# A hybrid streaming-encoder layer on one core: softmax normalisation moved from the probabilities to the outputs, and banded operands split by head pairs

## The chip, the cores and the metric

The kernel runs on one core of a Trainium2 chip. The metric is device microseconds (us) of one execution, lower is better; the times given are medians of several executions. The core has five engines with queues of their own: TensorE (PE; its weight loads are listed apart as PEld), VectorE (DVE), ScalarE (ACT), GpSimd (POOL) and SyncE (SP, which issues most transfers). They work at the same time and wait for one another through semaphores. SBUF and PSUM are the on-chip memories; TensorE writes to PSUM, in banks of 128 partitions by 512 float32.

## What is computed

One layer over 512 positions of width 1024, in float32, chunk-causal with chunks of 64. Three branches read one input projection: A is banded softmax attention with a clipped relative-position bias, B a gated linear recurrence (HGRN2), C multi-head latent attention. A and C have 8 heads with values of width 64. Their results are multiplied by a branch matrix, gated, summed and projected; a squared-ReLU feed-forward layer and a norm follow. The change touches the two softmaxes and the operands around them:

```python
# A, one chunk of queries
s = jnp.einsum('bqhd,bkhd->bhqk', q_blk, k_band).astype(jnp.float32) * scale + bias
s = jnp.where(valid[None, None], s, -jnp.inf)
p = jax.nn.softmax(s, axis=-1).astype(v.dtype)
return jnp.einsum('bhqk,bkhd->bqhd', p, v_band)
...
# C, one block of queries
s = (jnp.einsum('bqhd,bkhd->bhqk', qn, k_nope)
     + jnp.einsum('bqhr,bkr->bhqk', qr, k_rope)).astype(jnp.float32) * scale
s = jnp.where(mask[None, None], s, -jnp.inf)
p = jax.nn.softmax(s, axis=-1).astype(v.dtype)
return jnp.einsum('bhqk,bkhd->bqhd', p, v)
```

## The kernel before

**Precision.** An operand of a float32 product is split into a high part, rounded to the format that TensorE takes (`hi`, a copy on ScalarE), and a low part, the rest (`lo`, a subtraction on VectorE); `split` (L209) does both. A product is three matmuls, high by high, high by low and low by high (`mm3`, L223).

**Order of the work.** TensorE's order is written out by hand; the other engines' instructions are put in order by a planner that goes by the program's order and by what it expects to be ready, and each engine then takes its own in that order. The large projections are cut into units, mostly of one matmul, that wait in a list; `fill(n)` (L303) puts the next n units at that place of TensorE's order. Weights come by SyncE into two raw buffers (`load`, L261), are converted by ScalarE and an accumulating transfer (`convert`, L267), and two converted tiles are kept ahead (`get`, L283). The stages are: projection of the latent parts; attention C (span 66 to 158 us); attention A (to 280 us); the recurrence B, filled with the gate and branch matmuls (to 545 us); output projection and feed-forward.

**Attention** (L567) has one loop for both softmaxes, over 8 heads by 4 tiles of 128 queries, and a few steps more to drain. Step i of head h and tile t does, in TensorE's order: the scores of (h, t) (`scores_step`, L517), some fill, at odd steps a waiting value step (`value_step`, L555), the transposes of the tile two steps back (`transpose_step`, L541), the preparation of later operands, and fill again. The score step takes the row's minimum of the negated scores (VectorE, L526, or L530 with the bias added), and the exponential with its sum (ScalarE, L533). Its `norm` takes the reciprocal of the sum (L537) and scales the row of up to 512 probabilities (L538), both on VectorE. The transposes (L546) of the scaled row go to PSUM and are split into `pT`, which covers one head's 512 queries. The value step multiplies `pT` by the values, high parts and low parts of a head side by side (L562); the two halves of its 128 output rows are added by a copy (L564, ScalarE) and a sum (L565, VectorE) into one half of the tile `ys` of the head's pair. Value steps and transposes share two PSUM banks.

**Operands of attention C** are made from the latent projections by `prep_c` in stages (L673). Three of them, at L681, L686 and L691, write to the one PSUM bank called `up` (`pup`, L165): they fall on the steps of odd heads with t = 0, 1 and 2, heads 1, 3 and 5.

**Operands of attention A** are made by `prep_a(h)` (L790) at step (h - 2, 3). The scores of A have 64 rows of depth, so the high and low part of the query are stacked on 128 partitions (`q1`), against the high part of the keys twice (`k1`) and their low part twice (`k2`). Six operations on 64 partitions do this, three on ScalarE (L797, L799, L800) and three on VectorE (L798, L801, L802). The bias of the head is loaded by SyncE (L804), and made ready by VectorE (L805 to L807). The tiles `QT` rotate over four heads, `KT` over two.

**Natural values.** `project_nat` (L446) gives values with positions on partitions, for A (`avn`) and B (`bvn`), as four tiles of 128x512. In B, `ew_keys` (L1022) splits a head pair's values in four pieces of 128x128.

Of the kernel before, what the change touches and what calls it, by code (L numbers as in the profile page):

```python
# [9 lines left out]
F32 = mybir.dt.float32  # L10
F32R = mybir.dt.float32r
# [127 lines left out]
def _body(ctx, tc, ap, dbgo):  # L139
# [8 lines left out]
    def f(t):  # L148
        return t.bitcast(F32)
# [12 lines left out]
    def acc(n="acc"):  # L162
        return ps.tile([P, S], F32, tag="acc", name=n, bufs=3)
# [4 lines left out]
    def psc(n="sc"):  # L168
        return ps.tile([P, S], F32, tag="sc", name=n)
# [39 lines left out]
    def split(hi, lo, src):  # L209
        A.copy(hi, src)  # L210
        V.tensor_tensor(lo, src, f(hi), ALU.subtract)  # L211
# [122 lines left out]
    with ExitStack() as st_ctx:  # L334
# [111 lines left out]
        def project_nat(src, name, pool, out, halves=(0, 1)):  # L446

            def half_run(half):
                def run():
                    pz = [acc("pv").rearrange("p (a c) -> p a c", a=2) for _ in range(2)]  # L450
                    for k in range(NK):
                        if k % 4 == 0:
                            wh, wl = get()
                        c = slice(k % 4 * 256, k % 4 * 256 + 256)
                        for s in range(NST):
                            q = slice(s * P, (s + 1) * P)
                            mm3(pz[s // 2][:, s % 2], xg[k][0][:, q], xg[k][1][:, q], wh[:, c], wl[:, c],
                                k == 0 and s % 2 == 0, k == NK - 1, skip_group_check=True)
                            if s < 3 or k < NK - 1:
                                yield from (1, 1)[s % 2:]  # L460
                    for s in range(NST):
                        if half == 0:
                            out.append(pool[0].tile([P, S], F32, tag="nat", name=name, bufs=4))
# [50 lines left out]

    yraw = {}

    def scores_step(ab, t, scores, bias):  # L517
        n = (t + 1) * P
        sc = psc("sc")
        for i, (l, r) in enumerate(scores):  # L520
            T.matmul(sc[:, :n], l[:, t * P:(t + 1) * P], r[:, :n], start=i == 0, stop=i == len(scores) - 1)  # L521
        mn = ab.tile([P, 1], F32, tag="mn", name="mn", bufs=6)
        p = ab.tile([P, S], F32, tag="p", name="p", bufs=LAG + 1)
        if bias is None:
            V.memset(sc[0:64, n - 64:n], -NEG)
            V.tensor_reduce(mn, sc[:, :n], X, ALU.min)  # L526
# [6 lines left out]
        A.activation(p[:, :n], src[:, :n], AF.Exp, bias=mn, scale=-1.0, accum_out=sm)  # L533
        ri = ab.tile([P, 1], F32, tag="ri", name="ri", bufs=6)

        def norm():
            V.reciprocal(ri, sm)  # L537
            V.tensor_scalar(p[:, :n], p[:, :n], ri, None, ALU.mult)  # L538
        return p, norm

    def transpose_step(par, t, p, pT):  # L541
        n = (t + 1) * P
# [12 lines left out]
    def value_step(ab, h, v2, pT, y):  # L555
        par = h % 2
        av = ptp("av")
        for kt in range(NST):
            w = v2[kt][:, h, :]
            for i, x in enumerate(pT):  # L560
                r = x[:, kt, kt * P:] if par == 0 else x[:, 4 - kt, :(NST - kt) * P]
                T.matmul(av[:, kt * P:], w, r, start=kt == 0 and i == 0, stop=kt == NST - 1 and i == 1)  # L562
        lo = ab.tile([64, S], F32, tag="avl", name="avl", bufs=1)
        A.copy(lo, av[64:128])  # L564
        V.tensor_tensor(y[par * 64:(par + 1) * 64], av[0:64], lo, ALU.add)  # L565

    def attention(ab, ops, prep, v2, pT, ys, na, nb, nd, lag=LAG):  # L567


        pend, vals = [], []  # L570
        order = [(h, t) for h in range(8) for t in range(NST)]
        for i in range(len(order) + lag + 2):
            norm = None
            if i < len(order):
                h, t = order[i]
                p, norm = scores_step(ab, t, *ops(h))
                pend.append((h, t, p))
            fill(na[i % len(na)] if i < len(order) else nd)
            if vals and (i % 2 or i >= len(order)):
                h = vals.pop(0)  # L580
                value_step(ab, h, v2, pT, ys[h // 2])
            if len(pend) > lag or (i >= len(order) and pend):
                h, t, p = pend.pop(0)
                transpose_step(h % 2, t, p, pT)
                if t == NST - 1:
                    vals.append(h)
            if norm:
                norm()
            if i < len(order):
                prep(*order[i])  # L590
            fill(nb[i % len(nb)] if i < len(order) else nd)
        assert not pend and not vals

    with ExitStack() as at_ctx:
# [137 lines left out]
        with ExitStack() as a_ctx:  # L732
            app = a_ctx.enter_context(tc.tile_pool(name="apool", bufs=2, reuse_waits="tile"))
            v2 = []
            for s in range(NST):
                t = ab.tile([P, 8, P], F32R, tag="v2", name="v2a", bufs=4)
                split(t[:, :, 0:64], t[:, :, 64:128], avn[s].rearrange("p (h d) -> p h d", d=64))
# [49 lines left out]

            aops = {}

            def prep_a(h):  # L790
                pr, par = h // 2, h % 2
                q, k = aqk[2 * pr], aqk[2 * pr + 1]
# [4 lines left out]
                A.activation(q1[a], q[a], AF.Copy, scale=-SC_A)  # L797
                V.scalar_tensor_tensor(q1[o], q[a], -SC_A, f(q1[a]), ALU.mult, ALU.subtract)  # L798
                A.copy(k1[a], k[a])  # L799
                A.copy(k1[o], k[a])  # L800
                V.tensor_tensor(k2[a], k[a], f(k1[a]), ALU.subtract)  # L801
                V.tensor_copy(k2[o], f(k2[a]))  # L802
                bias = app.tile([P, S], F32, tag="bias", name="bias", bufs=2)
                nc.sync.dma_start(bias[:, 256:], ap['rel'][h])  # L804
                V.tensor_scalar(bias[:, 256:], bias[:, 256:], -1.0, None, ALU.mult)  # L805
# [14 lines left out]
    with ExitStack() as h_ctx:  # L820
# [103 lines left out]
        def items(pr):  # L924
# [356 lines left out]
```

## Time and profile before

| | |
|---|---|
| median of three executions | 983.39 us (981.54 to 986.31) |
| the profiled execution | 984.55 us |
| its span, first to last instruction | 982.8 us |
| mean granted TensorE clock | 0.98 of full speed |
| moved by DMA | 116 MB, mean 118 GB/s |

The profile shows one execution. Busy time of an engine counts its own instructions, not its waiting. A group line names the program line, engine, operation, tile written and tiles read, shape and count, then the busy time in us and the mean ns of one, and then the idle time of the engine just before them with what ended it. A wait line reads "engine tile line <- what it waited for: us in total, times, longest us". A timeline line has the start, the duration, and in brackets the idle time before it with its releaser. SPq and POOLq are instructions that issue transfers.

### The profile page before, as it was taken

Reading aid. Unit: us, or ns where it says so; the run is one execution under the profiler, and the core shown is the slowest. Engines: PE = TensorE matmul, PEld = TensorE weight load, DVE = VectorE, ACT = ScalarE, POOL = GpSimd, SP = SyncE. Lnnn points to the kernel's source line nnn. Section 1 sums busy time; section 2 is a strip of 40 time slices with the busy share of each in tenths; the row PEclk is TensorE's granted clock in tenths of the full one; section 3 lists DMA queues with packets and bytes.
Section 4 is the critical chain, followed back from the end, with each engine's and each line's share of the span. In section 5 each row is a group of like instructions: output and inputs, shape, how many; then the busy total and the mean of one; then the engine's idle time right before and its main releaser. Section 6 shows DMA issues by size and latency. Waiting matters only on the chain.

```text
span 982.8 us, 12692 instructions
## 1 busy us (share of the span) xinstructions
PE 932.0 (95%) x4682; PEld 782.3 (80%) x4682; DVE 598.0 (61%) x1136; ACT 547.9 (56%) x973; POOL 147.7 (15%) x182
## 2 busy tenths in 40 slices
PE   8799999998999999999999899999999999999995
PEld 6578798887878788777787678888888888888895
DVE  6788888777768869787462264544422234445845
ACT  7567778897777877777663444433322233432311
POOL 4211100001152324231111102100000000000032
PEclk9999999999999899999999999999999999999998
DMA  6554334455546474646587632232322222232402
GB/s 201 159 133 109 78 98 108 119 138 114 135 96 161 96 162 108 150 108 145 126 220 173 163 129 96 89 105 89 104 95 99 96 98 98 95 100 94 151 1 86
DMA packets 36894, 116.00 MB, mean 118 GB/s; under 512 B 4384, under 2 KB 8624, under 8 KB 36832
## 3 DMA queue, kind: packets, MB, share of 16 engines
q1 hardware_dynamic: 27840, 82.62, 26.5%
q0 software_dynamic: 8992, 32.56, 17.5%
q8 instruction: 37, 0.61, 0.3%
q14 instruction: 25, 0.20, 0.1%
HBM read 80.50 MB, written 2.16 MB: 84 GB/s over the span
## 4 chain that ended last, share of the span: by engine, by line
PE 54%; DVE 16%; ACT 13%; DMA 10%; issue 5%; POOL 1%; DVEq 0%; SPq 0%; ACTq 0%; POOLq 0%
PE p L224 12%; PE p L225 12%; PE p L226 12%; DMA wl<-wr 4%; DMA wr<-in_w_g 2%; ACT wl L275 2%; PE pj L320 2%; PE pj L322 2%; PE pj L324 2%; ACT wh L277 2%; DVE qbl L211 2%; PE po L225 1%; PE sc L521 1%; PE po L226 1%; PE po L224 1%
## 5 line engine op out<-in xcount | busy, mean ns | idle before, releaser
L220 DVE TENSOR_TENSOR wl<-wr,wh 128x1024 fp32r<-128x1024 f32 x66 | 80.8, 1224 | 146.2 <-ACT wh L219 146.2
L219 ACT CAST wh<-wr 128x1024 fp32r<-128x1024 f32 x66 | 69.5, 1052 | 174.4 <-PE p L225 138.6
L276 POOL DMA_DIRECT2D wl<-wr x62 | 53.8, 868 | 385.7 <-ACT wl L275 325.8
L277 ACT CAST wh<-wr 128x1024 fp32r<-128x1024 f32 x64 | 66.9, 1045 | 59.6 <-DMA wr<-in_w_g 19.0
L224 PE MATMUL p<-x2h,wh 128*128 128x512 f32 x256 | 100.0, 391 | 0.0
L226 PE MATMUL p<-x2h,wl 128*128 128x512 f32 x256 | 99.6, 389 | 0.0
L225 PE MATMUL p<-x2l,wh 128*128 128x512 f32 x256 | 99.6, 389 | 0.0
L224 PE MATMUL p<-rh,wh 128*128 128x512 f32 (+1 forms) x224 | 83.7, 374 | 0.0
L225 PE MATMUL p<-rl,wh 128*128 128x512 f32 (+1 forms) x224 | 83.7, 374 | 0.0
L226 PE MATMUL p<-rh,wl 128*128 128x512 f32 (+1 forms) x224 | 83.7, 374 | 0.0
L324 PE MATMUL pg<-xgh,wl 128*128 128x512 f32 x192 | 78.1, 407 | 5.1 <-DMA wl<-wr 5.1
L320 PE MATMUL pg<-xgh,wh 128*128 128x512 f32 x192 | 77.6, 404 | 0.0
L322 PE MATMUL pg<-xgl,wh 128*128 128x512 f32 x192 | 77.6, 404 | 0.0
L320 PE MATMUL pj<-xgh,wh 128*128 128x512 f32 x160 | 65.1, 407 | 1.9 <-ACT c L428 1.9
L322 PE MATMUL pj<-xgl,wh 128*128 128x512 f32 x160 | 65.7, 411 | 0.0
L275 ACT ACTIVATE wl<-wr 128x1024 fp32r<-128x1024 f32 x62 | 65.3, 1055 | 0.3
L324 PE MATMUL pj<-xgh,wl 128*128 128x512 f32 x160 | 64.4, 402 | 0.0
L1262 POOL TENSOR_TENSOR xres<-xres,cst 128x256 f32<-128x256 f32 x16 | 13.4, 838 | 335.4 <-ACT fss L1257 308.8
L224 PEld LDWEIGHTS p<-x2h,wh 128*128 128x128 f32 x256 | 48.1, 188 | 10.2 <-issue 0.2
L225 PEld LDWEIGHTS p<-x2l,wh 128*128 128x128 f32 x256 | 48.1, 188 | 10.1 <-issue 0.2
L226 PEld LDWEIGHTS p<-x2h,wl 128*128 128x128 f32 x256 | 48.1, 188 | 10.0
L324 PEld LDWEIGHTS pg<-xgh,wl 128*128 128x128 f32 x192 | 37.6, 196 | 13.9 <-DMA wl<-wr 6.4
(367 smaller groups left out, 2414.0 us busy)
## 6 DMA issues: line engine op xcount, KB each, us to landing
wr<-in_w_ff SPq DMA_DIRECT2D x64, 512.0 KB, 3.2
wl<-wr POOLq DMA_DIRECT2D x62, 512.0 KB, 4.8
wr<-in_w_g SPq DMA_DIRECT2D x24, 512.0 KB, 3.7
wr<-in_w_br SPq DMA_DIRECT2D x12, 512.0 KB, 3.8
wr<-in_w_aqk SPq DMA_DIRECT2D x8, 512.0 KB, 3.7
wr<-in_w_out SPq DMA_DIRECT2D x8, 512.0 KB, 3.2
xt<-in_xT SPq DMA_DIRECT2D x8, 256.0 KB, 4.3
wr<-in_w_av SPq DMA_DIRECT2D x4, 512.0 KB, 3.7
```

The source lines that it names most:

```text
L211: V.tensor_tensor(lo, src, f(hi), ALU.subtract)
L219: A.copy(hi[:, :n], r[:, :n])
L220: (eng or G).tensor_tensor(lo[:, :n], r[:, :n], f(hi[:, :n]), ALU.subtract)
L224: T.matmul(out, wh, xh, start=start, stop=False, **kw)
L225: T.matmul(out, wh, xl, start=False, stop=False, **kw)
L226: T.matmul(out, wl, xh, start=False, stop=stop, **kw)
L275: A.activation(lo, r, AF.Copy, scale=-1.0)
L276: G.dma_start(lo, r, accum_op=ALU.add)
L277: A.copy(hi, r)
L320: T.matmul(out, wh, xh, start=start, stop=False, **kw)
L322: T.matmul(out, wh, xl, start=False, stop=False, **kw)
L324: T.matmul(out, wl, xh, start=False, stop=stop, **kw)
```

## The change

1. `norm` per row is gone: the exponentials go to the transposes as they are, and their sums are kept for a head pair in `sums`, 128x4x2. After the value step of the pair's second head, VectorE takes one reciprocal of the eight columns, and ScalarE copies it, 64 times side by side for each head, to a 128x512 tile (`rw`), which shares its buffer with the copy of L564. At least three steps later four TensorE transposes turn it into rows in the bank `up`, and VectorE multiplies the pair's 128x512 output by them. The last pair's transposes stand behind the loop.
2. `prep_a` splits the queries and keys of a head pair at once, on 128 partitions, at the pair's first head (`split_a`). For each head six transfers of 64 partitions by 512 (128 KB), issued by SyncE ahead of the head's bias load, put the parts in their places in `q1`, `k1` and `k2`.
3. The natural values are one tile of 128x4x512 instead of four, and `ew_keys` splits a pair's values in one piece.

```diff
@@ scores_step, value_step, attention
+    sums = {}
-    def scores_step(ab, t, scores, bias):
+    def scores_step(ab, h, t, scores, bias):
+        if h % 2 == 0 and t == 0:
+            sums[h // 2] = ab.tile([P, NST, 2], F32, tag="sm", name="sm", bufs=3)
...
-        sm = ab.tile([P, 1], F32, tag="sm", name="sm", bufs=6)
-        A.activation(p[:, :n], src[:, :n], AF.Exp, bias=mn, scale=-1.0, accum_out=sm)
-        ri = ab.tile([P, 1], F32, tag="ri", name="ri", bufs=6)
-
-        def norm():
-            V.reciprocal(ri, sm)
-            V.tensor_scalar(p[:, :n], p[:, :n], ri, None, ALU.mult)
-        return p, norm
+        A.activation(p[:, :n], src[:, :n], AF.Exp, bias=mn, scale=-1.0, accum_out=sums[h // 2][:, t, h % 2:h % 2 + 1])
+        return p
...
         A.copy(lo, av[64:128])
         V.tensor_tensor(y[par * 64:(par + 1) * 64], av[0:64], lo, ALU.add)
+        if par:
+            ri = ab.tile([P, NST, 2], F32, tag="ri", name="ri", bufs=2)
+            V.reciprocal(ri, sums.pop(h // 2))
+            rw = ab.tile([P, NST, 2, 64], F32, tag="avl", name="rw", bufs=1)
+            A.copy(rw, ri.unsqueeze(3).to_broadcast([P, NST, 2, 64]))
+            def norm():
+                rb = pup("rb")
+                for t in range(NST):
+                    T.transpose(rb[:, t * P:(t + 1) * P], rw[:, t].rearrange("p a d -> p (a d)"), ident)
+                V.tensor_tensor(y, y, rb, ALU.mult)
+            return norm
...
                 h = vals.pop(0)
-                value_step(ab, h, v2, pT, ys[h // 2])
+                norm = value_step(ab, h, v2, pT, ys[h // 2])
+                if norm:
+                    norms.append((i, norm))
+            if norms and i > norms[0][0] + 2:
+                norms.pop(0)[1]()
...
-            if norm:
-                norm()
...
+        for _, norm in norms:
+            norm()
@@ prep_a
+            def split_a(pr):
+                q, k = aqk[2 * pr], aqk[2 * pr + 1]
+                qh, ql, kh, kl = late['a'] = [app.tile([P, S], F32R, tag="as", name=n, bufs=8)
+                                              for n in ("aqh", "aql", "akh", "akl")]
+                A.activation(qh, q, AF.Copy, scale=-SC_A)
+                V.scalar_tensor_tensor(ql, q, -SC_A, f(qh), ALU.mult, ALU.subtract)
+                split(kh, kl, k)
...
-                A.activation(q1[a], q[a], AF.Copy, scale=-SC_A)
-                V.scalar_tensor_tensor(q1[o], q[a], -SC_A, f(q1[a]), ALU.mult, ALU.subtract)
-                A.copy(k1[a], k[a])
-                A.copy(k1[o], k[a])
-                V.tensor_tensor(k2[a], k[a], f(k1[a]), ALU.subtract)
-                V.tensor_copy(k2[o], f(k2[a]))
+                nc.sync.dma_start(f(q1[a]), f(qh[a]))
+                nc.sync.dma_start(f(q1[o]), f(ql[a]))
+                for dst, src in ((k1, kh), (k2, kl)):
+                    nc.sync.dma_start(f(dst[a]), f(src[a]))
+                    nc.sync.dma_start(f(dst[o]), f(src[a]))
@@ project_nat, ew_keys
+                    if half == 0:
+                        w = pool[0].tile([P, NST, S], F32, tag="nat", name=name, bufs=1)
+                        out.append(w)
...
-                        A.activation(out[s][:, half * 256:half * 256 + 256], pz[s // 2][:, s % 2], AF.Copy,
+                        A.activation(out[0][:, s, half * 256:half * 256 + 256], pz[s // 2][:, s % 2], AF.Copy,
                                      scale=rstdn[:, s:s + 1])
...
-                for c in range(4):
-                    split(vh[:, c], vl[:, c], bvn[c][:, vs])
+                split(vh, vl, bvn[0][:, :, vs])
```

More of the change, by code (lines that the diff above doesn't have):

```diff
@@ L461, in run @@
                     for s in range(NST):
-                        if half == 0:
-                            out.append(pool[0].tile([P, S], F32, tag="nat", name=name, bufs=4))
-                        A.activation(out[s][:, half * 256:half * 256 + 256], pz[s // 2][:, s % 2], AF.Copy,
+                        A.activation(out[0][:, s, half * 256:half * 256 + 256], pz[s // 2][:, s % 2], AF.Copy,
                                      scale=rstdn[:, s:s + 1])
@@ L565, in value_step @@
         V.tensor_tensor(y[par * 64:(par + 1) * 64], av[0:64], lo, ALU.add)
+        if par:
[9 more added lines that the diff above has]
+            return norm
     def attention(ab, ops, prep, v2, pT, ys, na, nb, nd, lag=LAG):
-        pend, vals = [], []
+        pend, vals, norms = [], [], []
         order = [(h, t) for h in range(8) for t in range(NST)]
         for i in range(len(order) + lag + 2):
-            norm = None
             if i < len(order):
                 h, t = order[i]
-                p, norm = scores_step(ab, t, *ops(h))
-                pend.append((h, t, p))
+                pend.append((h, t, scores_step(ab, h, t, *ops(h))))
             fill(na[i % len(na)] if i < len(order) else nd)
@@ L736, in _body @@
                 t = ab.tile([P, 8, P], F32R, tag="v2", name="v2a", bufs=4)
-                split(t[:, :, 0:64], t[:, :, 64:128], avn[s].rearrange("p (h d) -> p h d", d=64))
+                split(t[:, :, 0:64], t[:, :, 64:128], avn[0][:, s].rearrange("p (h d) -> p h d", d=64))
                 v2.append(t)
@@ L788, in _body @@
             aops = {}
+            def split_a(pr):
[5 more added lines that the diff above has]
+                split(kh, kl, k)
             def prep_a(h):
                 pr, par = h // 2, h % 2
-                q, k = aqk[2 * pr], aqk[2 * pr + 1]
+                if par == 0:
+                    split_a(pr)
+                qh, ql, kh, kl = late['a']
                 a = slice(par * 64, par * 64 + 64)
```

## The prediction

> **What bounds the kernel now.** I read the page's busy times first, then busy time by stage, TensorE's waits in the two attention stages, and the timeline around the longest of them.
>
> ```profile
> PE 932.0 (95%) x4682; PEld 782.3 (80%) x4682; DVE 598.0 (61%) x1136; ACT 547.9 (56%) x973; POOL 147.7 (15%) x182
> ```
>
> ```profile
> 66.00:158.00 92.00, 88.86 (x535) 77.28 (x534) 77.86 (x211) 70.39 (x156) 12.36 (x12) 1.00 0.43 107
> 158.00:280.00 122.00, 112.22 (x665) 98.32 (x664) 91.83 (x265) 102.17 (x210) 14.65 (x20) 0.97 0.53 124
> 280.00:545.00 265.00, 250.60 (x1222) 207.66 (x1221) 182.15 (x324) 181.97 (x331) 69.41 (x95) 0.97 0.60 141
> ```
>
> The rows are latent attention, banded attention, and the recurrence with the gates; the columns are length, then busy PE, PEld, DVE, ACT, POOL, then clock, DMA share, GB/s. TensorE runs an order written out by hand and is busy 97% and 92% of the two attention stages, so it is the bound. VectorE (85% and 75%) and ScalarE (77% and 84%) matter only where TensorE waits for them:
>
> ```profile
> PE tp L546 <- DVE p L538: 3.8, 3, 2.0
> PE tp L546 <- DVE ya L565: 2.8, 2, 2.5
> PE av L562 <- ACT pTh L210: 2.4, 2, 1.6
> PE sc L521 <- ACT p L533: 1.3, 2, 0.7
> ...
> ```
>
> This is all that lighter VectorE and ScalarE can win here, beside the clock: about 10 us, 1% of the time. The 3.8 us are transposes waiting for the normalisation itself. The longest of the second row has another cause, in VectorE's, SyncE's and TensorE's timelines and the clock behind it:
>
> ```profile
> 221.84 0.29 DVE L805 TENSOR_SCALAR bias<-bias 128x256 f32<-128x256 f32 x1 [3.03 <-DMA bias<-in_rel]
> ```
>
> ```profile
> 218.00 0.33 SPq L264 DMA_DIRECT2D wr<-in_w_bq  x1
> 218.42 0.38 SPq L804 DMA_DIRECT2D bias<-in_rel  x1
> ```
>
> ```profile
> 222.92 0.55 PE L546 MATMUL tp<-ident,p 128*128 128x128 f32 x3 [2.53 <-DVE ya L565]
> ```
>
> ```profile
> 222.00:229.00 7.00, 6.08 (x25) 5.30 (x26) 5.10 (x18) 3.14 (x8) 0.01 (x1) 0.76 0.64 150
> ```
>
> A head's bias load went out 0.42 us behind a weight load. VectorE, which takes its work in order, stood 3.03 us at L805; the sum that frees the PSUM bank (L565) was queued behind it, and TensorE lost 2.53 us. The granted clock then averaged 0.76 over 7 us, another 7 x 0.24 = 1.7 us.
>
> **The change, part by part.** *Normalisation.* VectorE drops 64 reciprocals and 64 scalings:
>
> ```profile
> L538 DVE TENSOR_SCALAR p<-p,ri 128x128 f32<-128x128 f32 (+1 forms) x64 | 25.9, 405 | 1.2
> ...
> L537 DVE RECIPROCAL ri<-sm 128x1 f32<-128x1 f32 x64 | 10.1, 159 | 14.7 <-ACT p L533 14.4
> ```
>
> That is 36.0 us of VectorE. The transposes now read the exponentials directly, so the 3.8 us go entirely. In place come, for each of 8 head pairs, one reciprocal, a ScalarE broadcast copy, four TensorE transposes and a VectorE product. The transposes are of the form of L546:
>
> ```profile
> 154.99 0.60 PE L546 MATMUL tp<-ident,p 128*128 128x128 f32 x4
> ```
>
> One lasts 0.27 us, so four in a row step by (0.60 - 0.27)/3 = 0.11 us, and 32 cost 3.5 us of the bounding engine, which nothing hides. The Trainium skill (TensorE: Matmul & The Clock Gate, Part 4: PE-mode transpose) gives about 275 ns for one in a kernel's context. By that 32 would be 8.8 us, and the forecast 5.3 us later, 987.4; this trace agrees on the duration of one but shows them overlapping.
>
> The reciprocals wait in ScalarE's and VectorE's queues; the row transposes stand three steps later. A stage has 36 steps, so a step is 92/36 = 2.6 and 122/36 = 3.4 us, three are 7.7 and 10 us, and that hides reciprocal and broadcast (0.16 and some 0.6 us) except at two places. Without that cover each of the eight would cost TensorE the wait priced for the end, below.
>
> *First place: PSUM.* The rows go to the single bank that the latent projections (L681 to L692) use. A value step at odd step 11 puts its norm at step 14, between projection 2 of head pair 2 (step 13) and projection 3 (step 14); the same falls at step 22.
>
> ```profile
> 108.95 0.27 PE L546 MATMUL tp<-ident,p 128*128 128x128 f32 x1
> 108.98 0.48 PE L224 MATMUL pq<-cnh,cwh 128*128 128x512 f32 x1
> ```
>
> ```profile
> 109.14 0.56 DVE L526 TENSOR_REDUCE mn<-sc 128x1 f32<-128x384 f32 x1
> ```
>
> At step 14 the projection pq follows one transpose without a pause. Now it waits for the product that empties the bank. No row has that product; the 64x512 sum with a PSUM operand (L565, in the next rows) is 0.69 us and has as many columns. With the reduction of 0.56 us possibly ahead of it, a wait is 0 to 1.25 us. I take 0.85, nearer the upper end, because the reduction begins just as the rows would finish: 1.7 us for the two. While TensorE waits there, scores and fill stand behind it.
>
> *Second place: the end of banded attention,* where the schedule has no fill behind the last value step.
>
> ```profile
> 276.27 0.41 PE L562 MATMUL av<-pTl,v2a 128*128 128x128 f32 x1
> ...
> 276.73 0.58 ACT L564 COPY avl<-av 64x512 f32<-64x512 f32 x1 [2.73 <-PE av L562]
> ...
> 277.33 1.28 ACT L936 ACT_TABLE_LOAD   x1
> 277.34 0.69 DVE L565 TENSOR_TENSOR ya<-av,avl 64x512 f32<-64x512 f32 x1 [2.62 <-ACT avl L564]
> ```
>
> TensorE now has to stand through copy 0.58, sum 0.69 and broadcast copy (like the first, 0.58; the tile shares its buffer, so it waits for the sum), with hops of 0.05: 2.0 us. If the table load goes in between it is up to 3.3; the lower end is 1.3, should the clock recover while TensorE stands (the matmuls of these rows run at twice their usual times). I take 2.0, which the rows give one by one. The gate matmuls, and all of the recurrence, are queued behind it. The latent stage has fill there and pays nothing; without that fill it would pay the same 2.0.
>
> *Banded operands.* Rows of all that reads the projection:
>
> ```profile
> L797 ACT ACTIVATE qt<-aqk x8: 617/633/644, 149.4 to 224.0; 64x512 fp32r<-64x512 f32 x8
> L799 ACT CAST kt<-aqk x8: 611/617/624, 149.9 to 244.0; 64x512 fp32r<-64x512 f32 x8
> L798 DVE SCALAR_TENSOR_TENSOR qt<-aqk,qt x8: 684/687/689, 150.1 to 224.6; 64x512 fp32r<-64x512 f32 x8
> L801 DVE TENSOR_TENSOR kt<-aqk,kt x8: 662/683/691, 150.9 to 245.3; 64x512 fp32r<-64x512 f32 x8
> L800 ACT CAST kt<-aqk x8: 618/619/621, 152.3 to 244.6; 64x512 fp32r<-64x512 f32 x8
> ```
>
> ScalarE had 1.87 us a head, 15.0 in all; now a pair takes 1.25 (same columns on twice the partitions), 5.0 in all. VectorE's two go from 11.0 to 5.5. What is moved goes to SyncE: six copies of 128 KB a head, ahead of that head's bias load, and ahead of the weight loads that follow. A copy that overwrites a key tile waits for the scores that read it, now on SyncE instead of ScalarE. The first scores of a head come four steps, 14 us, after that, against six issues of 0.33 and a landing like that of the bias, also 128 KB:
>
> ```profile
> DMA to landing us min/median/max: 2.0/3.1/4.5
> ```
>
> So the scores do not wait (2.0 + 4.5 = 6.5 us); without those steps between, each head would wait up to that. A weight load held back by 2 us is covered by the tiles that the planner keeps ahead, two raw and two converted: none of the waits above is for a weight. Uncovered, it would be 2 us a head. The bias load is the weak spot, below.
>
> *One tile for the natural values.* Four splits of 128x128 a pair become one of 128x512:
>
> ```profile
> L210 ACT CAST vh<-bvn x16: 287/294/299, 279.7 to 437.4; 128x128 fp32r<-128x128 f32 x16
> L211 DVE TENSOR_TENSOR vl<-bvn,vh x16: 276/285/756, 288.8 to 438.3; 128x128 fp32r<-128x128 f32 x16
> ```
>
> ScalarE 4.7 to about 2.5 us, VectorE 4.6 to 2.7. Of TensorE's waits in the recurrence
>
> ```profile
> PE sl L224 <- ACT kxh L210: 3.7, 3, 1.8
> PE sl L224 <- DVE sT L967: 3.2, 2, 1.8
> ```
>
> I give a tenth, 0.7 us, since only 12 of 324 and 12 of 331 operations of that stage go. Bounds: 0 and half of them.
>
> **Sum.** Off: 3.8 (normalisation); half of the L565 waits, 1.4, and half of the clock loss, 0.85, since they hang on one bias load; 0.4 of the ScalarE split waits (1.6 of the 2.4 are the tail's chain, which stays); 1.3 of waits on the exponential, whose minimum was queued behind the scalings; 0.7 in the recurrence: 8.45 us. On: 3.5 + 1.7 + 2.0 = 7.2 us. Net 1.25 us faster. The profiled execution took 984.55 us (span 982.8 and 1.75 around it), 1.16 above the median of 983.39; set against the median the forecast is **982.1 us**, by its own bounds 977 to 988.
>
> **Rivals.** *The relief passes on in full (faster).* VectorE loses 34.7 us net in the attention stages (36.0 and 5.5 off; 5.5 of products and 1.3 of reciprocals on), ScalarE 5. If that empties their queues, all listed waits but the tail's 1.6 go, the clock stays up, half of the recurrence's rows go, and the product follows the rows at once: 3.8 + 2.8 + 1.7 + 0.8 + 1.3 + 3.5 = 13.9 off, 3.5 + 2.0 on: 975.0. For it speaks VectorE's 85%; against it, the bias load and chains whose length is latency.
>
> *The bias load behind six copies (slower).* It leaves SyncE 2.0 us later than now. Where VectorE reaches L805 before it lands, all of VectorE stands. A stand of 3.03 cost TensorE 2.53, so the first 0.5 us is free; 2.0 us at six heads (2 to 7) is 6 x 1.5 = 9.0, and the 2.25 that I credited above is not won: 993.4. It decides from the point where L805's place in VectorE's order is earlier than the landing by over 0.5 us. For it: two of eight already wait, 3.8 us in all, and L804 shows 2.0 to 4.5 us to land. Against it: six of eight do not, and a planner that moves L805 later pays nothing. The Trainium skill (DMA: Bandwidth & Descriptors, Rules for kernel authors) says that transfers to disjoint partition halves serialize, and to use one of 128 partitions instead; its SBUF page (SBUF — State Buffer, Door 1) has 196 GB/s for 64 partitions. By that, an estimate, six copies take 4.0 us and the six heads 21, some 1005 us. No run here shows a 64-partition copy.
>
> *The waits only move.* Only the 3.8 us go, because the others are latencies: 7.2 - 3.8 = 3.4 slower, 986.8.
>
> **Chances.** Forecast 0.40, full relief 0.27, bias load 0.20 (the page's 1005 within it, 0.03), waits moved 0.13 (with it the 987.4 of slower transposes, 0.03). About 0.5% (4.9 us) can be told from no change here: below 978.5, above 988.3. Faster: 0.9 of full relief and a quarter of the forecast, 0.35. Slower: nearly all of the bias load, some of the moved waits and of the forecast, 0.26. No change: 0.39. The range, 972 to 993, leaves out half of the bias load and the far end of full relief.
>
> **What would show it.** Right: no wait on a DVE line ahead of L546's lines except L565's; 32 more transposes at 0.11 us; a wait of about 2 us ahead of the last four; waits ahead of pq at steps 14 and 22. Wrong: VectorE idle on the bias load at most heads, or waits ahead of the scores on the copies.

## The result and the profile after

The changed kernel takes 1000.07 us, median of four executions (997.19 to 1001.65), against 983.82 for the kernel before beside it (981.54 to 986.31): a ratio of 1.0161, 95% interval 1.0127 to 1.0195. It is slower by 16 us. The forecast was 982.1 with a range of 972 to 993, so the result lies outside it on the slow side. The profiled execution of the changed kernel took 997.19 us (span 995.4), the lowest of its four; its trace accounts for 12.6 of the 16 us.

First, where the time is lost. These rows of TensorE's timeline are the same instruction in both kernels, first before, then after:

```profile
159.97 0.40 PE L562 MATMUL av<-pTh,v 128*128 128x512 f32 x1
...
183.79 0.36 PE L224 MATMUL pv<-wh,xgh 128*128 128x256 f32 x1
...
283.67 0.39 PE L320 MATMUL pg<-xgh,wh 128*128 128x512 f32 x1
```

```profile
161.86 0.40 PE L561 MATMUL av<-pTh,v 128*128 128x512 f32 x1
...
193.60 0.36 PE L224 MATMUL pv<-wh,xgh 128*128 128x256 f32 x1
...
289.55 0.41 PE L561 MATMUL av<-pTl,v2a 128*128 128x128 f32 x1
...
300.34 0.39 PE L320 MATMUL pg<-xgh,wh 128*128 128x512 f32 x1
```

The delay is 1.9 us at the last value step inside the latent loop, 9.8 us a few steps into banded attention, 13.3 at its last value matmul (the prediction shows 276.27 for it before), and 16.7 in the gate matmuls behind it. By the end of the span 12.6 are left. So the passage from one attention stage to the other costs 7.9 us, the middle of the banded stage 3.5, its end 3.4, the latent loop 1.9; the recurrence and what follows give 4.1 back.

TensorE's waits in both stages, after:

```profile
PE tp L545 <- DVE pTl L211: 5.4, 3, 2.9
PE av L561 <- ACT pTh L210: 5.1, 2, 3.5
PE rb L575 <- ACT rw L570: 4.3, 2, 2.2
PE pq L224 <- DVE yc L576: 2.4, 2, 1.2
PE tp L545 <- DVE bias L832: 2.2, 1, 2.2
```

The 3.8 us ahead of the transposes are gone, as forecast, and the page's VectorE line went from 598.0 us to 565.1, ScalarE's from 547.9 to 540.8. In their place stand new waits. The third and fourth rows are the normalisation's own: the row transposes (`rb`) wait for their broadcast at two places, the projection `pq` for the product at two. The first, second and fifth rows have other causes, which the timeline of the passage shows (SyncE, ScalarE and TensorE), and behind it the clock, in the column after the busy times:

```profile
162.19 0.93 SPq L827 DMA_DIRECT2D kt<-akh  x1
...
167.27 0.62 ACT L210 CAST akh<-aqk 128x512 fp32r<-128x512 f32 x1 [3.00 <-DMA kt<-akh]
...
170.27 0.79 PE L561 MATMUL av<-pTh,v 128*128 128x512 f32 x1 [3.49 <-ACT pTh L210]
...
175.41 1.12 PE L575 MATMUL rb<-ident,rw 128*128 128x128 f32 x4 [2.23 <-ACT rw L570]
```

```profile
164.00:171.00 7.00, 3.51 (x26) 2.83 (x24) 2.86 (x5) 4.00 (x9) 0.00 (x0) 0.88 0.96 230
171.00:178.00 7.00, 4.77 (x16) 4.13 (x16) 4.62 (x7) 4.82 (x9) 0.86 (x1) 0.50 0.54 110
```

ScalarE takes its work in order. The planner has put the split of the third head pair (`akh`) ahead of ScalarE's last latent work, though the program has it at step (2, 3) of the banded stage. Its tile has eight buffers, two pairs of four, and the first pair's are still read by a copy that SyncE issued at 162.19. ScalarE stands 3.00 us; `pTh`, queued behind it, comes late, TensorE stands 3.49 us, then 2.23 more ahead of `rb`, and has half its clock for 7 us.

The middle of the banded stage is read from VectorE's and SyncE's waits, and from the timeline around one of them:

```profile
DVE bias L830 <- DMA bias<-in_rel: 11.0, 4, 3.5
...
DVE akl L211 <- DMA kt<-akl: 5.9, 1, 5.9
```

```profile
SPq L826 <- PE sc L526: 26.8, 5, 11.0
```

```profile
244.31 2.44 SPq L827 DMA_DIRECT2D kt<-akl  x1
...
248.84 0.33 SPq L264 DMA_DIRECT2D wr<-in_w_bq  x1
...
249.27 0.38 SPq L829 DMA_DIRECT2D bias<-in_rel  x1
...
252.84 0.29 DVE L830 TENSOR_SCALAR bias<-bias 128x256 f32<-128x256 f32 x1 [3.12 <-DMA bias<-in_rel]
...
253.75 0.30 PE L545 MATMUL tp<-ident,p 128*128 128x128 f32 x1 [2.23 <-DVE bias L832]
```

A copy into a key tile waits for the scores that read it; it waits on SyncE, up to 11.0 us, and whatever SyncE has behind it waits too. Two of VectorE's four stands on the bias load come behind such copies, which had waited 11.0 and 5.4 us for scores. The other two come behind weight loads that had waited 6.3 and 2.0 us for their raw buffer. The stand shown here is one of these: from 241.42 on SyncE issues four key copies, the last of them for 2.44 us, then waits 2.0 us for the weight load's buffer, and the bias load goes out at 249.27. VectorE stands 3.12 us on it, and TensorE 2.23 us on VectorE. A weight load is what held the bias load in the prediction's rows, too (218.00 and 218.42): SyncE had waited 9.0 us ahead of it.

### The profile page after: what moved, and what is told of

Same layout as the page of the kernel before. It is cut to its first block, busy times and chain, and to the rows that moved or that the text cites. A ratio compares the mean times of both kernels' runs of the same rounds, so it can differ in the third digit from the quotient of the medians.

```text
span 995.4 us, 12715 instructions
## 1 busy us (share of the span) xinstructions
PE 938.3 (94%) x4714; PEld 788.7 (79%) x4714; DVE 565.1 (57%) x996; ACT 540.8 (54%) x953; POOL 150.3 (15%) x182
## 4 chain that ended last, share of the span: by engine, by line
PE 63%; ACT 11%; DMA 10%; DVE 9%; issue 5%; SPq 1%; POOL 1%; DVEq 0%; ACTq 0%; POOLq 0%
PE p L224 12%; PE p L225 12%; PE p L226 12%; DMA wl<-wr 4%; DMA wr<-in_w_g 2%; PE pj L320 2%; PE pj L322 2%; ACT wl L275 2%; PE pj L324 2%; PE pg L324 2%; PE pg L322 2%; PE pg L320 2%; PE po L225 2%; PE po L226 2%; PE po L224 2%
## 5 line engine op out<-in xcount | busy, mean ns | idle before, releaser
L226 PEld LDWEIGHTS p<-rh,wl 128*128 128x128 f32 x224 | 42.2, 188 | 7.5
```

What stands on the lines that cost most here:

```text
L226: T.matmul(out, wl, xh, start=False, stop=stop, **kw)
```

## The experiments

Ratios are to the kernel before, run beside them on the same chip (medians 984.2 to 985.1); us are of the median.

| kernel | what it is | us | ratio, 95% interval |
|---|---|---|---|
| e1_norm | normalisation (part 1) alone | 989.57 | 1.0061, 1.0031 to 1.0090 |
| e2_copies | banded operands (part 2) alone | 988.84 | 1.0037, 1.0014 to 1.0061 |
| e4_late | after, ScalarE's splits later | 994.29 | 1.0092, 1.0058 to 1.0127 |
| e5_bias | after, bias load ahead of copies | 1000.57 | 1.0160, 1.0118 to 1.0201 |
| e6_bias3 | after, three bias buffers | 997.70 | 1.0133, 1.0100 to 1.0165 |
| e10_bias53 | e5 and e6 together | 998.33 | 1.0150, 1.0113 to 1.0186 |
| e15_after_pool | after, bias operations on GpSimd | 993.30 | 1.0075, 1.0043 to 1.0106 |
| e13_late_bias | e4, e5 and e6 together | 993.88 | 1.0111, 1.0069 to 1.0153 |
| e7_ends | e1 without its own waits | 980.58 | 0.9964, 0.9938 to 0.9990 |
| e8_bias | e7, three bias buffers | 982.56 | 0.9971, 0.9950 to 0.9991 |
| e9_before_bias3 | before, three bias buffers | 984.66 | 1.0008, 0.9982 to 1.0035 |
| e11_all | e13 and e7 together | 984.67 | 1.0009, 0.9988 to 1.0030 |
| e12_ends_nat | e7 and the single tile (part 3) | 981.23 | 0.9968, 0.9942 to 0.9994 |
| e16_best_pool | e12, bias operations on GpSimd | 981.75 | 0.9969, 0.9949 to 0.9989 |
| e14_all_pool | e11, bias operations on GpSimd | 978.66 | 0.9937, 0.9912 to 0.9962 |
| e17_step14 | e14, `rb` three steps later again | 985.13 | 0.9990, 0.9965 to 1.0014 |
| e18_ends_back | e14, stage ends as in the change | 983.99 | 0.9999, 0.9972 to 1.0027 |

**The parts alone.** e1 has the changed `scores_step`, `value_step` and `attention`, and the rest of the kernel before; e2 has the changed `prep_a` and nothing else.

```diff
e1, against after:
-                nc.sync.dma_start(f(q1[a]), f(qh[a]))
...
+                A.activation(q1[a], q[a], AF.Copy, scale=-SC_A)
...
e2, against after:
-        return p
+        def norm():
+            V.reciprocal(ri, sm)
+            V.tensor_scalar(p[:, :n], p[:, :n], ri, None, ALU.mult)
+        return p, norm
...
```

> The change without its second and third part: softmaxes normalised on the outputs, operands of banded attention and natural values as before. Theory 1 (the stacking copies are the larger cost: ScalarE and VectorE, which take their work in order, stand at buffers and bias loads that wait for copies): 3 to 6 us slower than the kernel before. Theory 2 (the normalisation's own waits are the cost: 3.5 us of transposes, 2.4 ahead of pq, 4.3 ahead of the row transposes at the two ends): 9 to 13 us slower.

> The kernel before with the second part alone: operands of banded attention split by pairs and stacked by transfers. Theory 1: 8 to 12 us slower than the kernel before, with VectorE idle on the bias load and ScalarE idle on the landing of copies. Theory 2: within 3 us of the kernel before.

Both parts lose, by 6.0 and 3.6 us (ratio less one, times 984; so in what follows), and neither theory had the sizes: the copies alone are the smaller loss, and the whole change loses 15.8, which is 6 more than the sum. In e1's trace (of its longest execution, 7 us above the median) the normalisation's own waits stand as in the change; in e2's VectorE's stands on the bias load, and TensorE behind VectorE (of these waits the kernel before has 3.8 and 0.2 us):

```profile
PE rb L574 <- ACT rw L569: 4.6, 2, 2.6
...
PE pq L224 <- DVE yc L575: 2.4, 2, 1.2
```

```profile
DVE bias L816 <- DMA bias<-in_rel: 14.5, 4, 7.7
```

```profile
PE tp L546 <- DVE pTl L211: 9.8, 5, 5.2
```

**ScalarE's stand at the passage.** e4 orders the splits of the third and fourth pair, on ScalarE, behind the exponential of the step that makes them, (2, 3) and (4, 3).

```diff
-                A.activation(qh, q, AF.Copy, scale=-SC_A)
+                first = A.activation(qh, q, AF.Copy, scale=-SC_A)
+                if pr >= 2:
+                    after(first, late['exp'])
```

> The changed kernel, but the planner may not put the splits of the third and fourth head pair (the ones that reuse buffers which copies still read) before the exponential of the step at which the program has them. If the 7.9 us lost at the end of latent attention come from ScalarE standing at such a split (3.0 us in the trace, 3.5 on TensorE, then the clock), this takes 5 to 8 us off the changed kernel: 8 to 11 us slower than the kernel before. If that stand only shows a wait that would come anyway (theory 2), within 2 us of the changed kernel.

A hit: 15.8 us over the kernel before become 9.1. In its trace no wait of ScalarE for a copy is left in the banded stage, and the waits ahead of `av` are back about where the kernel before had them (2.4):

```profile
PE av L561 <- ACT pTh L210: 2.6, 2, 1.6
```

VectorE's 5.9 us stand on `akl`, the low part of the fourth pair's keys, is gone as well, so e4 prices the two together.

**VectorE's stands on the bias load: three tries that missed, and one that took them away.**

```diff
e5, against after:
+                bias = app.tile([P, S], F32, tag="bias", name="bias", bufs=2)
+                nc.sync.dma_start(bias[:, 256:], ap['rel'][h])
                 nc.sync.dma_start(f(q1[a]), f(qh[a]))
...
-                bias = app.tile([P, S], F32, tag="bias", name="bias", bufs=2)
-                nc.sync.dma_start(bias[:, 256:], ap['rel'][h])
e6, against after; e10 has both:
-                bias = app.tile([P, S], F32, tag="bias", name="bias", bufs=2)
+                bias = app.tile([P, S], F32, tag="bias", name="bias", bufs=3)
e15, against after:
-                V.tensor_scalar(bias[:, 256:], bias[:, 256:], -1.0, None, ALU.mult)
-                V.tensor_scalar(bias[:, :256], relc[:, h:h + 1].to_broadcast([P, 256]), -1.0, None, ALU.mult)
-                V.memset(bias[0:64, S - 64:S], -NEG)
+                G.tensor_scalar(bias[:, 256:], bias[:, 256:], -1.0, None, ALU.mult)
+                G.tensor_scalar(bias[:, :256], relc[:, h:h + 1].to_broadcast([P, 256]), -1.0, None, ALU.mult)
+                G.memset(bias[0:64, S - 64:S], -NEG)
```

> The changed kernel with a head's bias load issued ahead of its six copies instead of behind them. If VectorE's stands on the bias load (11.0 us in four waits) cost TensorE time, as the slower rival of the prediction had it: 3 to 6 us off the changed kernel, and those waits go. If not: within 2 us of the changed kernel, 16 us slower than the kernel before.

> The changed kernel with three bias buffers in place of two, so that a head's bias load can go out a head earlier and land before VectorE gets to it. Theory A (copies make VectorE stand on the bias load, and TensorE pays for the stand): VectorE's waits on the bias load, 11.0 us in four, fall below 2 us, and the time falls by 3 to 6 us against the changed kernel, to 994-997. Theory B (VectorE's stands are covered by its new slack; the stands that cost are ScalarE's, at the split of the third pair, and the new transposes' own waits): the waits on the bias go too, but the time stays within 1.5 us of the changed kernel's 1000.1.

> The changed kernel with both limits on the bias load taken away: it is issued ahead of the head's six copies and has three buffers. Each alone left VectorE's waits for it where they were (14.8 and 12.2 us) and the time within 2.4 us of the changed kernel, since the other limit remained. Theory A (these waits cost TensorE time in the middle of the banded stage): the waits fall below 3 us and the time is 3 to 7 us below the changed kernel's 1000.1, so 993-997. Theory B (they are covered by VectorE's slack): the waits go and the time stays within 2.5 us of 1000.

> The changed kernel with only the three bias operations moved to GpSimd. Theory A (VectorE's stands on the bias load cost TensorE time in the middle of the banded stage): 3 to 6 us below the changed kernel's 1000.1, 994 to 997. Theory B (they cost nothing): within 2 us of it.

e5, e6 and e10 take off 0.1, 2.8 and 1.1 us, inside their intervals. Read by the time alone that is Theory B or near it, and it would have been wrong: the waits that they were to remove are still there, 14.8, 12.2 and 10.8 us. e10's waits of VectorE, then of SyncE, say why:

```profile
DVE bias L830 <- DMA bias<-in_rel: 10.8, 4, 3.6
```

```profile
SPq L828 <- PE sc L526: 27.2, 5, 10.9
```

SyncE still stands 27.2 us on the copies into the key tiles (L828 is the first of these in e10), and a load put ahead of one head's copies is behind the head before's. Nor does the third buffer give VectorE more time. In the changed kernel the bias operation that stands 3.52 us at 195.60 is the third head's, whose first scores VectorE takes at 204.59. In e10 the planner has moved these operations a head forward as well: the one that stands 3.38 us at 196.50 is the fourth head's, whose first scores come at 221.25. No run here holds VectorE's operation back instead. Only e15 takes the stand off VectorE, by letting GpSimd stand instead: 8.4 us less than the change (1.61% to 0.75% over the kernel before), more than Theory A had. TensorE's wait on L832 is gone from its trace; one long one, of another cause, stays: 4.6 us at 212.09, behind a VectorE that stood 7.42 us for a split tile (`akl`) that a copy was still reading.

> The changed kernel with the bias load freed as in e10_bias53, and the splits of the third and fourth pair ordered on ScalarE behind the exponential of the step before, as in e4_late (994.3). Theory A (two separate stands of two engines, both paid for): 987 to 991, what is left over the kernel before being the normalisation's own waits. Theory B (only ScalarE's stand costs): 992 to 996, as e4_late.

e13 is e4 with the two edits that did not work, and measures the same as e4: Theory B by number, for the reason just told. Against e10, which lacks only e4's edit, it is 3.8 us less (1.50% to 1.11%), a second and smaller price for ScalarE's stand.

**The normalisation's own waits.** e7 takes them away in e1: the row transposes come a step later, ahead of the value step, where no latent projection follows; the reciprocal, and in the banded stage the broadcast, are made before the value matmuls; the latent stage's last `rb` stand behind the first fill of the banded one.

```diff
+            if norms and i > norms[0][0] + 3:
+                norms.pop(0)[1]()
             if vals and (i % 2 or i >= len(order)):
                 h = vals.pop(0)
...
-            if norms and i > norms[0][0] + 2:
-                norms.pop(0)[1]()
...
             fill(TUNE['a0'])
+            for norm in rest:
+                norm()
```

> The normalisation alone (no copies, no single tile of values), with its own waits taken away: the row transposes stand a step later, where nothing of the latent projections is behind them; the reciprocal is taken, and in the banded attention the broadcast made in a buffer of its own, before the value matmuls; the last transposes of the latent attention stand behind the first fill of the banded one. Theory A (the normalisation's cost is its four waits, two at the stages' ends with the lower clock behind them, two ahead of the latent projections): 6.0 us over the kernel before turns into 3 us less to 1 more than it. Theory B (the waits only move, and the 32 transposes with a displaced order cost by themselves): 3 to 7 us over the kernel before, as with the normalisation alone.

Theory A, and half a microsecond beyond its range: from 6.0 us over the kernel before to 3.5 under it.

> All of the change with every stand found so far taken away: e13_late_bias, with the row transposes a step later, the last ones behind the banded stage's first fill, and the last pair's broadcast made before its value matmuls, as in e7_ends. Theory A (the causes add): 977 to 983, at or below the kernel before. Theory B (the copies cost something else that no stand shows): 985 or more.

e11 makes the same edits in e13 (there only the last banded broadcast is made early), and takes off as much: 1.11% to 0.09%. At 984.67 it lies between the two theories, 1.7 us above the one and 0.3 below the other: something of the copies was left.

> The kernel of e11_all (984.7) with the three bias operations of each head on GpSimd in place of VectorE, so that GpSimd and not VectorE waits for the bias load. Theory A (VectorE's 15 us of stands on the load are what the copies still cost): TensorE's waits on the low part of the transposed rows, 6.9 us in four, fall below 3, and the time is 3 to 5 us below e11_all, 980 to 982. Theory B (the rest is traffic and the copies' latency): within 1.5 us of 984.7.

It was the stands on the bias load. With GpSimd taking them (26.1 us in four in its trace) the full change measures 978.66, 0.63% below the kernel before and the fastest here. Of TensorE's waits on the low part of the transposed rows 6.9 us are left at 1.0; now some scores wait for their copies:

```profile
PE tp L545 <- DVE pTl L211: 6.9, 4, 4.1
```

```profile
PE sc L526 <- DMA kt<-akh: 2.2, 1, 2.2
PE tp L545 <- DVE pTl L211: 1.0, 2, 0.6
PE sc L526 <- DMA kt<-akl: 0.9, 1, 0.9
```

e17 and e18 put the two kinds of wait back into e14, one at a time.

```diff
e17, against e14:
-            if norms and i > norms[0][0] + 3:
-                norms.pop(0)[1]()
...
+            if norms and i > norms[0][0] + 2:
+                norms.pop(0)[1]()
e18, against e14:
+        for _, norm in norms:
+            norm()
...
-            for norm in rest:
-                norm()
...
```

> The kernel of e14_all_pool (978.7) with the row transposes three steps after the value step again, as the change has them, so that two of them stand right ahead of a latent projection. Theory A (each of the two waits, 1.2 us in the trace, is lost in full): 2 to 4 us above 978.7. Theory B (the forecast's 0.85 each): 1 to 2 us above. Theory C (the fill makes them up): no difference.

> The kernel of e14_all_pool with the ends of both attention stages as the change has them: reciprocal and broadcast behind the value step, the last row transposes right behind the loop. Theory A (both ends cost, the latent one as much as the banded one, with a lower clock behind them): 4 to 7 us above 978.7. Theory B (the forecast: 2.0 at the banded end and nothing at the latent one): 1.5 to 2.5 us above.

Each kind costs the whole gain, 5.2 and 6.1 us by the ratios; since each ratio is known to some 2.5 us, each difference is known to some 3.5 to 4. In e17 the two waits are 1.2 us each again, and its latent loop ends 3.1 us later than e14's: they are lost in full, Theory A. The 5.2 us lie above that theory's 2 to 4, and nothing here shows where the rest is lost. For e18 the end of the banded stage in TensorE's timeline and three windows of busy times, first of e14, then of e18, show what the stands cost; the windows are 163 to 170, 170 to 177 and 275 to 283 us, the clock the third number from the right:

```profile
274.86 0.28 PE L571 MATMUL av<-pTl,v2a 128*128 128x128 f32 x1
274.98 0.62 PE L583 MATMUL rb<-ident,rw 128*128 128x128 f32 x4
275.35 0.48 PE L320 MATMUL pg<-xgh,wh 128*128 128x512 f32 x1
...
281.57 0.39 PE L320 MATMUL pg<-xgh,wh 128*128 128x512 f32 x1
```

```profile
163.00:170.00 7.00, 5.26 (x30) 3.95 (x29) 3.92 (x7) 6.91 (x13) 0.86 (x1) 1.00 0.96 211
170.00:177.00 7.00, 7.00 (x46) 6.38 (x45) 3.07 (x9) 3.91 (x9) 0.00 (x0) 1.00 0.38 111
275.00:283.00 8.00, 8.00 (x40) 6.70 (x39) 6.23 (x11) 6.36 (x11) 7.50 (x13) 1.00 0.48 114
```

```profile
167.99 1.12 PE L575 MATMUL rb<-ident,rw 128*128 128x128 f32 x4 [2.59 <-ACT rw L570]
...
274.39 0.41 PE L561 MATMUL av<-pTl,v2a 128*128 128x128 f32 x1
276.84 1.11 PE L575 MATMUL rb<-ident,rw 128*128 128x128 f32 x4 [2.04 <-ACT rw L570]
277.61 0.78 PE L320 MATMUL pg<-xgh,wh 128*128 128x512 f32 x1
...
286.27 0.39 PE L320 MATMUL pg<-xgh,wh 128*128 128x512 f32 x1
```

```profile
163.00:170.00 7.00, 3.78 (x15) 3.08 (x16) 4.66 (x7) 5.43 (x9) 0.85 (x1) 0.77 0.95 216
170.00:177.00 7.00, 7.00 (x27) 5.71 (x27) 0.73 (x4) 0.67 (x3) 0.00 (x0) 0.74 0.29 81
275.00:283.00 8.00, 6.16 (x17) 5.01 (x18) 5.60 (x10) 5.43 (x11) 6.05 (x12) 0.51 0.26 82
```

From the last value matmul to the first gate matmul it is 0.49 us in e14 and 3.22 in e18, 2.7 more. From there to the same later gate matmul, the last row of each, it is 6.2 and 8.7 us: another 2.4, which is the clock (0.51). It had already fallen at e18's value matmul (0.41 us against 0.28), ahead of the stand, and did not come back while TensorE stood. So the stand did not make it fall, and 2.4 is the upper end of what the stand cost in clock. In e11, which has e14's stage ends and no wait there, the clock had fallen too, and the same stretch takes 7.4 us:

```profile
280.05 0.78 PE L320 MATMUL pg<-xgh,wh 128*128 128x512 f32 x1
...
287.42 0.39 PE L320 MATMUL pg<-xgh,wh 128*128 128x512 f32 x1
```

In the kernel before it is 7.2, in the changed kernel 7.6.

At the latent end the wait is 2.59 us and the clock 0.77 and 0.74 over 14 us. There the clock goes with the stand: in the traces of e1, e4, e13 and e18, which have it, the mean clock of the 8 us behind the last latent value matmul is 0.59 to 0.79; in those of the kernel before, e7, e11, e14 and e17, which do not, it is 1.00. From that matmul to the same projection matmul behind it, e18 takes 4.7 us more than e14. Both ends cost, Theory A.

**Controls.** e8, e9 and e12 give e7, the kernel before and e7 one edit each; e16 gives e12 the GpSimd edit.

```diff
e8 against e7, e9 against before:
-                bias = app.tile([P, S], F32, tag="bias", name="bias", bufs=2)
+                bias = app.tile([P, S], F32, tag="bias", name="bias", bufs=3)
e12 against e7:
-                for c in range(4):
-                    split(vh[:, c], vl[:, c], bvn[c][:, vs])
+                split(vh, vl, bvn[0][:, :, vs])
```

> The kernel of e7_ends with three bias buffers. Theory A (VectorE, lighter now, stands on the bias load, and TensorE pays): 2 to 4 us below e7_ends, so 1 to 6 us below the kernel before. Theory B (the stands are covered): within 1.5 us of e7_ends.

> The kernel before with three bias buffers and nothing else. In its profile one stand of 3.03 us on the bias load cost TensorE 2.53 us and lowered the clock behind it for some 1.7 us more. Theory A (that stand is paid for): 2 to 4 us below the kernel before. Theory B (it is made up later, since the order has other waits there): within 1.5 us of it.

> The kernel of e7_ends (the normalisation without its own waits: 980.6) with the single tile of natural values added, no copies. Theory A (the third part of the change is worth at most a microsecond, as the forecast had it): within 1.5 us of 980.6. Theory B (ScalarE and VectorE, relieved by some 4 us in the recurrence, let TensorE gain half of its waits there): 2 to 4 us below it.

> The normalisation without its own waits and the single tile of natural values, no copies (981.2), with the bias operations on GpSimd. Here VectorE stood on the load for 3.6 us in three. Theory A: 1 to 2 us below, about 980. Theory B: within 1 us.

None moves the time by more than its interval. The single tile of values is worth under what can be measured, as the forecast had it. Without copies the bias operations are not worth moving (e16), so it is not the lighter VectorE by itself that wins 7.1 to 8.4 us in e14 and e15. e9 is inconclusive: in its trace a stand of 3.0 us on the bias load remained, so it does not tell what that stand is worth.

## Why the prediction was wrong

*What held.* The 3.8 us ahead of the transposes went. The row transposes cost what was said (four in 0.60 to 0.66 us where TensorE has its clock). The wait at the end of the banded stage is 2.04 us (2.0 forecast). The relief was of the right size in sum: 8.45 us off less 3.5 for the transposes would be 5.0 faster without new waits, and e14, with most of the new waits taken away, is 6.2 faster (3.7 to 8.7). No run shows that it was so term by term; the list of what VectorE loses left out one operation, L802, 0.42 us eight times. The single tile is small.

*First failed step: "The latent stage has fill there and pays nothing."* It has none. At that point the list of units is used up: between the last latent value matmul and `rb` TensorE has nothing, and waits 2.2 to 2.6 us, as at the other end. The prediction's own clause, without that fill it would pay the same 2.0, was the true case.

*Second: the waits were priced without the clock.* The forecast charged 1.7 us of clock to the 2.53 us stand of before, and none to the stands that the change adds. At the latent end it fell with the stand; at the banded end, where it falls in the kernel before too, the changed kernel loses 3.0 us by the wait and the transposes and 0.4 by the clock. In all, the four waits cost 9.5 to 10 us (e1 to e7, e13 to e11) where the sum had 3.7. The waits ahead of `pq` were 1.2 us each, inside the bounds but above the 0.85 taken.

*Third, the copies were priced by their issue: "2.0 us later than now", and for the forecast at nothing beside half of the L565 waits.* The prediction named that a copy into a key tile would now wait on SyncE, and then asked only whether its own scores would be late. They were not, in the changed kernel. What was late was everything else that depends on those copies: VectorE's bias operations, behind a SyncE that stands up to 11.0 us, and the buffers of the split operands, which stay taken until the copies have read them, so that ScalarE stood at the third pair's split. The first is the effect that the rival given 0.20 named, VectorE standing on a late bias load, priced at 9.0 us and the 2.25 not won; moving the stand to GpSimd wins 7.1 to 8.4. The size is right, the way to it is not: that rival had the load late by the copies' 2.0 us of issue, at six heads, where the trace has four stands, behind SyncE's waits of 2.0 to 11.0 us. The rival's 1005, the nearest number on record, is near by chance: it charges 21 us to the bias load alone, two to three times what moving the stand wins. The second, 3.8 us (e10 to e13) to 6.7 (after to e4), was in no rival. Its precondition, eight buffers for four tiles a pair, stood in the diff.

*The account.* From the changed kernel by e10, e13 and e11 to e14 the time goes from 15.8 us over the kernel before to 14.8, 10.9, 0.9 and 6.2 under: 1.1 for the loads, 3.8 for ScalarE's stand, 10.0 for the normalisation's waits, 7.1 for VectorE's stands. Steps of one chain add up by construction. What tests them is that the last three, measured from other kernels, come out at 6.7 (after to e4), 9.5 (e1 to e7) and 8.4 (after to e15): 24.6 in place of 20.9, the same within the intervals. The normalisation alone also beats the kernel before once its waits are gone (e7, e12), and no run tells whether the copies add to that: e14's interval and e12's overlap. Why e1 and e2 together lost 6 us more than their sum is not shown by a run of its own; ScalarE's stands at these splits, 1.4 us in e2 and 5.3 in the change, are a likely part of it.

## What to carry to other kernels

When work goes from an engine to a transfer, price three things beside its issue: how long the issuing queue stands on the destination's readers and what is queued behind it, how long the source buffers stay taken, and which in-order engine meets either one. A wait put at the end of a stage costs its length, and can cost the clock behind it; look for the fill that is meant to hide it in the trace, at that place. And where an experiment is to take a wait away, read in its trace that the wait has gone before its time is taken for a verdict: here three did not take it away, in part because the planner moved the waiting operation along with the load.

## What the runs showed of the hardware that was not expected

The granted clock falls after shorter stands than thought. With a stand of 2.59 us, and one of 1.03 shortly before it, e18's mean over 14 us was 0.75; with stands of 1.04 and 0.47 at the same place e14 kept 1.00. At the banded end it fell after less, and not every time: over the 7 us up to the last value matmul, with a stand of 1.56 us and others of at most 0.63, the mean is 1.00 in e14 and 0.80 in e17. The Trainium skill (TensorE: Matmul & The Clock Gate, Part 1: The HAM clock gate) has the clock fall after an idle window of about 3.4 us; no single stand of e18 or e17 there was so long. No run here gives the rule.

An instruction that issues a transfer lasts up to 2.4 us in a row of them. Here are the low key part's second copy and the bias load of the changed kernel, with the durations in ns, minimum, median and maximum:

```profile
L827 SPq DMA_DIRECT2D kt<-akl x8: 587/791/2437, 154.8 to 258.7; - x8
```

```profile
L829 SPq DMA_DIRECT2D bias<-in_rel x8: 327/539/2447, 138.0 to 259.4; - x8
```

The prediction had 0.33 us for each. From issue to landing the second copies into the key tiles (L827) took 2.3, 4.9 and 7.4 us (minimum, median, maximum). A bias load of the same 128 KB took 2.3, 4.1 and 5.8 beside them, and 2.0, 3.1 and 4.5 in the kernel before. This is the row of the copies:

```profile
DMA to landing us min/median/max: 2.3/4.9/7.4
```
